# Moving the first attention head's weighted sum from its own period to the period that follows, in a hybrid retention and sparse-attention block

## The chip, the cores and the metric

The kernel runs on one core of one Trainium2 chip. The metric is the time of one execution on the device, in microseconds (us). A profile is one execution recorded by the hardware profiler; its span is the time from its first to its last recorded instruction.

## The reference

One block of a model with 512 tokens, 16 meta tokens ahead of them (528 in all), and 1024 channels, in float32: a gated feed-forward part, a mixer, another gated feed-forward part, and a final norm. The mixer projects its normed input once and feeds two branches, retention with 4 heads and sparse attention with 8 heads of width 128; sigmoid gates merge them. The change lies in the attention branch, which for each head is, cut to what matters:

```python
# per query: the 16 meta tokens, and the 128 keys that an indexer ranks highest
s_meta = einsum('bqhd,bmhd->bhqm', qb, k_meta) * scale
s_sel  = einsum('bqhd,bqkhd->bhqk', qb, k_sel) * scale      # masked where not allowed
p = softmax(concatenate([s_meta, s_sel], axis=-1))
out = einsum('bhqm,bmhd->bqhd', p[..., :16], v_meta) + einsum('bhqk,bqkhd->bqhd', p[..., 16:], v_sel)
```

The queries and keys get a rotary embedding (rope) first. The selection is made once for all heads and stands in the kernel as an additive bias on the scores.

## The kernel before

**Number format and matmuls.** Every float32 operand of a matmul is split into a high part and a low part in a reduced format: ACT (ScalarE) copies the source into the high part, and DVE (VectorE) subtracts it from the source for the low part (`split`, L117 and L118). A product is then three matmuls: high x high, high x low, low x high. Weights go through the same split when they arrive from memory: `raw` is the loaded tile (two buffers), `whi` and `wlo` are its parts (three buffers, used in turn), so a weight split must wait until the matmuls that read the buffer before are done. `mm3` (L157) is the matmul loop of all projections.

**Periods.** The attention branch is one Python loop over eight heads, `for h in range(AH)`. One pass of it is called a period here. In period h TensorE (PE) does, in this order:

1. for h > 0, the scores of head h: 15 matmuls into `psS` (L1970). DVE adds the bias and takes the row maximum (L1973), ACT takes the exponential (L1976), DVE normalises the result in place (`pj`, L1980 and L1981);
2. the query projection (`psaq`) and the key projection (`psak`) of head h + 1. ACT, DVE and POOL (GpSimd) apply rope (L1292 to L1296), and ACT and DVE split the result into `aq` and `ak`, which the scores of the next period read;
3. for h from 2 to 7, the weighted sum of head h - 1 (`weigh_turned`, into `psao`, L2028 and L2029);
4. a projection tile of a gate (`wide_gate`, into `psgate` or `psga`), which has nothing to do with the heads.

**Two ways to turn the probabilities.** The weighted sum needs them with keys on the partitions. For heads 1 to 6, DVE transposes blocks (`turn`), POOL writes them to memory (`pd`), SP (SyncE) reads them back (`land`), and ACT and DVE split them into the parts `pth` and `ptl` (`turned_parts`); this takes so long that the sum comes one period later. Heads 0 and 7 take `transpose_p`: PE transposes into four one-bank PSUM tiles `psPT` (L2037, L2039), and ACT and DVE split those straight into the same buffers `pth` and `ptl`. The 16 rows of the meta tokens go apart into `ptail` (L1367 to L1371). Each of these part buffers exists once.

**Head 0 and head 7.** In period 0 the order on PE is: the two projections of head 1, the transposes of head 0, a gate tile, and then head 0's weighted sum (`weigh_v`: 13 matmuls, L1537 and L1538, and a split into the head's output). Period 7 has the transposes of head 7, a gate tile, and head 7's weighted sum in the same way. `weigh_v` and `weigh_turned` differ in the layout of the parts that they read and write. The output of a head overwrites that head's values in the tile `vo`.

**PSUM.** `sm_tile` has four one-bank tiles, used by `psS` (three of the four score tiles), `psaq`, `psPT` and some gate tiles. `mm_tile` has two two-bank tiles, used by the fourth score tile, `psak`, `psao` and the other gate tiles.

**What sets the order.** PE runs in source order throughout, by `tc.manual_schedule(engines={PE})`. ACT, DVE, POOL and the DMA queues are ordered when the kernel is built, by a planner that fills each engine from the instructions that its own model of the time holds ready, those earlier in the source first. Every engine then works through its queue in that fixed order.

Of the kernel before, what the change touches and what calls it, by code (L numbers as in the profile page):

```python
# [33 lines left out]
AH = 8  # L34
# [47 lines left out]
def kernel(ctx: ExitStack, tc: tile.TileContext, x, meta, g1, wg1, wu1, wd1, gm,  # L82
# [11 lines left out]
    def pool(name, bufs=1, space=None, side=None):  # L94
        kw = {} if space is None else {"space": space}
        if side is not None:
            kw["side"] = side
        return tc.tile_pool(name=name, bufs=bufs, reuse_waits="tile", **kw)
# [17 lines left out]
    def split(src, hi, lo, eng=nc.vector):  # L116
        nc.scalar.activation(hi, src, AF.Copy)  # L117
        eng.tensor_tensor(lo, src, hi.bitcast(F32), ALU.subtract)  # L118
# [459 lines left out]
    def sm_tile(name):  # L578
        return mx["sm"].tile([P, S], F32, tag="sm", name=name)

    def mm_tile(name):
        return mx["mm"].tile([P, 1024], F32, tag="mm", name=name)
# [770 lines left out]
    def split_values(raw, parts):  # L1353

        for c in (0, 2):
            split(raw[:, c : c + 2], *(p[:, c : c + 2, :] for p in parts))
        return [(parts[0][:, c, :], parts[1][:, c, :], tp["v"][:TR, c * P : (c + 1) * P]) for c in range(4)]

    def place_tails(i):

        for r, part in ((0, 0), (32, 0), (64, 1)):
            nc.gpsimd.dma_start(tp["v"][r : r + NM].bitcast(F32).rearrange("q (c d) -> q c d", c=4),
                                vd[i, part].rearrange("(c q) d -> q c d", q=32)[:NM])

    def split_rows(src, t, order):

        nc.scalar.activation(t[:NM], src, AF.Copy)  # L1367
        at = [32 * i for i in range(1, 3) if order[i] == "h"][0]
        nc.scalar.activation(t[at : at + NM], src, AF.Copy)
        at = 32 * order.index("l")  # L1370
        nc.vector.tensor_tensor(t[at : at + NM], src, t[:NM].bitcast(F32), ALU.subtract)  # L1371
# [26 lines left out]
    if True:  # L1398
# [132 lines left out]
        def weighted(ps, vb, prob):  # L1531

            for kb in range(4):
                vh, vl = (part[:, kb * P : (kb + 1) * P] for part in vb[:2])
                ph, pl = prob[kb]
                for i, (a, b) in enumerate(((vh, ph), (vh, pl), (vl, ph))):
                    nc.tensor.matmul(ps[:, KQ[kb] :], a, b, start=kb == 0 and i == 0, stop=False)  # L1537
            nc.tensor.matmul(ps[:, KQ[4] :], vb[2], tp["p"][:TR, :NM], start=False, stop=True)  # L1538
# [371 lines left out]
    with pool("ao") as ao:  # L1910
        vo = [ao.tile([P, AH, S], F32R, tag=f"vo{i}", name="vo") for i in range(2)]
        ao_parts = [(vo[0][:, c, :], vo[1][:, c, :]) for c in range(AH)]
        with pool("at") as at:
# [21 lines left out]
            def proj_q(w=None):  # L1935
                w = w or cq.next()
                ps = sm_tile("psaq")
                mm3([(ps, REAL)], w, xs, KD)
                return rope_q(ps)
# [7 lines left out]
            def proj_k():  # L1947
                w = ck.next()
                parts, ps = halves(mm_tile("psak"))
                mm3(parts, w, xs, KD)  # L1950
                return rope_k(ps)
# [33 lines left out]
            def scores(q, k):  # L1985
                for j in (2, 1, 0, 3):
                    score(j, q, k)()

            def part_tiles(kb, n):
                return [at.tile([P, S - Q0[kb]], F32R, tag=f"pt{c}{kb}", name=f"pt{c}")[:, :n] for c in "hl"]  # L1990

            def turn(h):

                for j in (2, 1, 0, 3):
                    m = min(-(-(NM + P * (j + 1)) // 32), 16)
                    nc.vector.transpose(cross[:, :m, j, :], prob[j][:, : 32 * m].rearrange("p (b k) -> p b k", k=32))
                nc.vector.transpose(crosst, prob[3][:, S : S + 32])
                d = pd[h % 2]
                for a in range(4):
                    nc.gpsimd.dma_start(d.rearrange("(b i) a c -> a i b c", i=32)[a],  # L2000
                                        cross[32 * a : 32 * a + 32].rearrange("p b j c -> p b (j c)"))
                nc.gpsimd.dma_start(land[4], crosst[96 : 96 + NM, NM:])
# [6 lines left out]
            def turned_parts():  # L2009
                parts = []  # L2010
                for kb, q0 in enumerate(Q0):
                    ph, pl = part_tiles(kb, S - q0)
                    split(land[kb], ph, pl)
                    parts.append((ph, pl))
                split_rows(land[4], tp["p"][:, :NM], "hlh")
                return parts

            def weigh_turned(h, parts, v):

                ps = mm_tile("psao")[:, :S]  # L2020
                for kb, q0 in enumerate(Q0):
                    vh, vl = (part[:, kb * P : (kb + 1) * P] for part in v[:2])
                    ph, pl = (part.rearrange("p (a c) -> p a c", a=4) for part in parts[kb])
                    o = ps.rearrange("p (a c) -> p a c", a=4)[:, :, q0 // 4 :]
                    if q0 == 0:
                        (ph, pl), o = parts[kb], ps
                    for i, (a, b) in enumerate(((vh, ph), (vh, pl), (vl, ph))):
                        nc.tensor.matmul(o, a, b, start=kb == 0 and i == 0, stop=False)  # L2028
                nc.tensor.matmul(ps[:, KQ[4] :], v[2], tp["p"][:TR, :NM], start=False, stop=True)  # L2029
                split(*(t.rearrange(f"p ({o}) -> p a j c", a=4, j=4) for o, t in zip(("a j c", "j a c", "j a c"), (ps, *ao_parts[h]))))  # L2030

            def transpose_p():
                parts = []
                for kb in range(4):
                    ps = sm_tile("psPT")
                    for j in range(max(kb - 1, 0), 4):
                        nc.tensor.transpose(ps[:, j * P : (j + 1) * P], prob[j][:, kb * P : (kb + 1) * P], ident)  # L2037
                    if kb == 3:
                        nc.tensor.transpose(ps[:NM, 0:P], prob[3][:, 4 * P : T], ident)  # L2039
                    n = S - KQ[kb]  # L2040
                    ph, pl = part_tiles(kb, n)
                    if kb == 3:
                        split_rows(ps[:NM, P - NM : P], tp["p"][:, :NM], "hlh")
                    split(ps[:, KQ[kb] :], ph, pl)
                    parts.append((ph, pl))
                return parts

            def weigh_v(h, parts, v):
                ps = mm_tile("psao")[:, :S]
                weighted(ps, v, parts)  # L2050
                split(ps, *ao_parts[h])

            def wide_gate(tile=None):
                if gr.at < gr.n:
                    gate_acc(KD - gr.n + gr.at, gate(gr, at, wide=tile is None))
                else:
                    t = gate_a(tile or mm_tile("psga")[:, :S])
                    nc.sync.dma_start(gd[KD + ga.at - 1], t)

            place_tails(4)  # L2060
            with tc.manual_schedule(engines=BUSY):
# [12 lines left out]
                vs = split_values(raw, [v[:, :4, :] for v in vo])  # L2074
                raw = fetch_values(5, vraw())
            pend = None
            for h in range(AH):
                more = h + 1 < AH
                if h:
                    scores(q, k)  # L2080
                if more:
                    q, k = proj_q(w if h == 0 else None), proj_k()
                else:
                    wide_gate(sm_tile("psga"))
                    wide_gate()
                if pend is not None:
                    weigh_turned(h - 1, pend, vs[h - 1])
                    pend = None
                if h == 0:
                    with tc.manual_schedule(engines=BUSY):  # L2090
                        vs += split_values(raw, [v[:, 4:, :] for v in vo])
                    vrs.close()
                    crp = crs.enter_context(pool("cross", 1, side="right"))
                    cross = crp.tile([P, 16, 4, 32], F32, tag="cross", name="cross")
                    for j in range(3):
                        nc.gpsimd.memset(cross[:, 4 * j + 5 :, j, :], 0.0)
                if 0 < h and more:
                    turn(h)
                    wide_gate(sm_tile("psga"))
                    turned(h)  # L2100
                    pend = turned_parts()
                else:
                    pt = transpose_p()
                    wide_gate()
                    weigh_v(h, pt, vs[h])
                if h == 4:
                    place_tails(5)

        crs.close()

# [32 lines left out]
    with pool("om") as ou:  # L2143
# [10 lines left out]
        pend = []  # L2154
        for c in range(KD):
# [5 lines left out]
            if len(pend) == 2:  # L2161
                to_tokens(pend)
                pend = []
            nc.vector.tensor_tensor(hc, ps, hc, ALU.add)
            h, l = new_x(c)
# [248 lines left out]
```

## Time and profile before

| what | value |
|---|---|
| median of 3 runs | 1512.89 us (1512.02 to 1515.25) |
| the profiled execution's own time | 1512.66 us |
| its span | 1510.8 us |
| PE busy | 1498.6 us |
| DVE busy | 1113.5 us |
| ACT busy | 729.9 us |
| POOL busy | 122.2 us |
| mean granted PE clock | 0.997 |
| the loop over the heads, about | 892 to 1068 us of the span |

The rows shown below come from views of this one profiled execution. In the chain of waits a row has a start, a length, and the engine, tile and line that the end of the kernel hung on in that stretch. In the timeline a row has a start, a length, engine, line, operation, output and inputs with their shapes, how many instructions were merged (x), and in brackets the idle time of the engine ahead of it and what ended that. In the windows each stretch has its length and the busy time of each engine, then the granted PE clock, the share of time that the DMA engines were busy, and GB/s. All times are in us from the start of the span.

### The profile page before, as it was taken

The page shows a single profiled execution, that of the slowest core. Times are in us where ns is not written, and L with a number is a line of the kernel's source. Part 1 is how long each engine was busy: PE and PEld are TensorE (multiplying, and loading weights), DVE is VectorE, ACT ScalarE, POOL GpSimd, SP SyncE. Part 2 cuts the span into 40 slices and gives each one's busy share as a digit, 9 for nine tenths or more (in the row PEclk, how much of TensorE's full clock was granted, in tenths as well). Part 3 has the DMA queues.
Part 4 walks back from the last instruction along what each step waited for, and adds up shares of the span by engine and source line. Part 5 has one row for each costly group of instructions (what it writes and reads, how often), then busy time and mean ns, then how long its engine had stood idle before and what let it go on. Part 6 is the DMA issues. An engine that isn't in the chain of part 4 may idle for free.

```text
span 1510.8 us, 23879 instructions
## 1 busy us (share of the span) xinstructions
PE 1498.6 (99%) x9664; PEld 1361.2 (90%) x9664; DVE 1113.5 (74%) x1740; ACT 729.9 (48%) x1134; POOL 122.2 (8%) x169
## 2 busy tenths in 40 slices
PE   9999999999999999999999998999999999999998
PEld 8999999999988888888898887988888899899996
DVE  4988585786786768678978887787455888586675
ACT  5555263454354444443333356677345445254453
POOL 1000000002111120000000132331001000000000
PEclk9999999999999999999999999999999999999999
DMA  5232323226544444232322244566443223233232
GB/s 170 64 121 87 116 92 112 86 96 200 205 149 168 167 146 158 87 122 72 117 93 87 95 130 134 154 189 193 147 135 124 84 84 110 86 112 112 84 117 93
DMA packets 161918, 184.90 MB, mean 122 GB/s; under 512 B 12048, under 2 KB 130344, under 8 KB 161168
## 3 DMA queue, kind: packets, MB, share of 16 engines
q1 hardware_dynamic: 151056, 156.70, 32.3%
q0 software_dynamic: 5920, 17.68, 3.5%
q10 hardware_dynamic: 4832, 9.00, 1.7%
q8 instruction: 76, 1.25, 0.3%
q14 instruction: 34, 0.28, 0.1%
HBM read 161.05 MB, written 22.30 MB: 121 GB/s over the span
## 4 chain that ended last, share of the span: by engine, by line
PE 97%; DVE 1%; ACT 1%; issue 1%; DMA 0%; POOL 0%; POOLq 0%; DVEq 0%; ACTq 0%
PE psqX L157 14%; PE psd L157 8%; PE psd L2249 8%; PE psqY L157 7%; PE psrg L157 6%; PE psro L157 6%; PE psvX L1181 4%; PE psqZ L157 3%; PE psrk L157 3%; PE psu L157 3%; PE psrq L157 3%; PE psga L157 3%; PE psat L157 3%; PE psmo L157 3%; PE psak L157 3%; PE psaq L157 3%
## 5 line engine op out<-in xcount | busy, mean ns | idle before, releaser
L329 ACT ACTIVATE whi<-raw 128x1024 fp32r<-128x1024 f32 (+2 forms) x184 | 169.5, 924 | 129.0 <-PE psd L157 37.5
L330 DVE TENSOR_TENSOR wlo<-raw,whi 128x1024 fp32r<-128x1024 f32 (+2 forms) x184 | 198.6, 1083 | 40.6 <-ACT whi L329 40.5
L157 PE MATMUL psqX<-th,whi 128*128 128x264 f32 (+1 forms) x432 | 122.3, 283 | 0.0
L157 PE MATMUL psqX<-tl,whi 128*128 128x264 f32 (+1 forms) x432 | 122.3, 283 | 0.0
L157 PE MATMUL psqX<-th,wlo 128*128 128x264 f32 (+1 forms) x432 | 122.2, 283 | 0.0
L329 ACT ACTIVATE whi<-wsum 128x1024 fp32r<-128x1024 f32 x72 | 76.3, 1060 | 70.7 <-PE psd L2249 22.0
L117 ACT ACTIVATE whi<-raw 128x1024 fp32r<-128x1024 f32 (+1 forms) x60 | 62.2, 1043 | 86.0 <-PE psat L157 26.6
L330 DVE TENSOR_TENSOR wlo<-wsum,whi 128x1024 fp32r<-128x1024 f32 x72 | 87.8, 1221 | 12.5 <-ACT whi L329 12.5
L118 DVE TENSOR_TENSOR wlo<-raw,whi 128x1024 fp32r<-128x1024 f32 (+1 forms) x60 | 73.6, 1228 | 28.3 <-ACT whi L117 27.4
L157 PEld LDWEIGHTS psqX<-th,whi 128*128 128x128 f32 x432 | 82.1, 190 | 0.1
L157 PEld LDWEIGHTS psqX<-tl,whi 128*128 128x128 f32 x432 | 82.0, 190 | 0.0
L157 PEld LDWEIGHTS psqX<-th,wlo 128*128 128x128 f32 x432 | 82.0, 190 | 0.0
L157 PE MATMUL psro<-vo,whi 128*128 128x512 f32 x256 | 78.7, 389 | 0.0
L157 PE MATMUL psd<-hl,whi 128*128 128x264 f32 x352 | 71.3, 284 | 0.0
L157 PE MATMUL psd<-hh,wlo 128*128 128x264 f32 x352 | 70.8, 283 | 0.0
L157 PE MATMUL psd<-hh,whi 128*128 128x264 f32 x352 | 70.7, 282 | 0.0
L2249 PE MATMUL psd<-wlo,hh 128*128 128x512 f32 (+1 forms) x182 | 69.2, 382 | 0.0
L2249 PE MATMUL psd<-whi,hh 128*128 128x512 f32 (+1 forms) x182 | 69.2, 382 | 0.0
L2249 PE MATMUL psd<-whi,hl 128*128 128x512 f32 (+1 forms) x182 | 69.2, 382 | 0.0
L157 PEld LDWEIGHTS psro<-vo,whi 128*128 128x128 f32 x256 | 48.0, 188 | 10.1 <-DVE vo L330 0.2
L157 PEld LDWEIGHTS psd<-hh,wlo 128*128 128x128 f32 x352 | 54.5, 188 | 0.0
L157 PEld LDWEIGHTS psd<-hh,whi 128*128 128x128 f32 x352 | 54.2, 188 | 0.0
(476 smaller groups left out, 4540.8 us busy)
## 6 DMA issues: line engine op xcount, KB each, us to landing
raw<-in_ffn_w_up_dram SPq DMA_DIRECT2D x22, 1024.0 KB, 5.0
raw<-in_ffn_w_gate_dram SPq DMA_DIRECT2D x21, 1024.0 KB, 5.0
raw<-in_w_in_dram SPq DMA_DIRECT2D x18, 1024.0 KB, 5.0
raw<-in_w_in_dram SPq DMA_DIRECT2D x33, 512.0 KB, 3.8
raw<-in_ffn_w_down_dram SPq DMA_DIRECT2D x24, 512.0 KB, 4.4
w<-in_w_in_dram SPq DMA_DIRECT2D x24, 512.0 KB, 6.1
raw<-in_ffn_w_down_dram SPq DMA_DIRECT2D x12, 768.0 KB, 4.4
raw<-in_w_ret_out_dram SPq DMA_DIRECT2D x8, 1024.0 KB, 4.8
```

Of the source, the lines that this page charges most:

```text
L117: nc.scalar.activation(hi, src, AF.Copy)
L118: eng.tensor_tensor(lo, src, hi.bitcast(F32), ALU.subtract)
L157: nc.tensor.matmul(o, a[:, k, :], b[:, sl], start=first and k == 0 and i == 0, stop=last and k == nk - 1 and i == 2, skip_group_check=onto)
L329: nc.scalar.activation(hi, src, AF.Copy)
L330: return lambda: nc.vector.tensor_tensor(lo, src, hi.bitcast(F32), ALU.subtract)
L1181: nc.tensor.matmul(d[bank_][t], a, b[:, k, :], start=not onto and j + k + m == 0, stop=j + k == 3 and m == 2, skip_group_check=onto)
L2249: nc.tensor.matmul(ps, a[:, bs], m[:, j, cs], start=first and i == 0, stop=last and i == 2)
```

## The change

The parts that `transpose_p` returns in period 0 are no longer used at once; they are kept in `pend`, as the parts of heads 1 to 6 are. In period 1 `weigh_v` for head 0 then stands where `weigh_turned` stands in the later periods: behind the scores of head 1 and the two projections of head 2, ahead of the transposes by DVE and the gate tile. Head 7 keeps its place: its sum is now written behind the loop, and PE reaches it behind the same gate tile as before.

```diff
                 if pend is not None:
-                    weigh_turned(h - 1, pend, vs[h - 1])
-                    pend = None
+                    (weigh_turned, weigh_v)[h == 1](h - 1, pend, vs[h - 1])
...
                     pend = turned_parts()
                 else:
-                    pt = transpose_p()
+                    pend = transpose_p()
                     wide_gate()
-                    weigh_v(h, pt, vs[h])
                 if h == 4:
                     place_tails(5)
+            weigh_v(AH - 1, pend, vs[AH - 1])
```

## The prediction

> **What bounds the kernel now.** I read the page first, for the engine that sets the time.
>
> ```profile
> span 1510.8 us, 23879 instructions
> PE 1498.6 (99%) x9664; PEld 1361.2 (90%) x9664; DVE 1113.5 (74%) x1740; ACT 729.9 (48%) x1134; POOL 122.2 (8%) x169
> PE 97%; DVE 1%; ACT 1%; issue 1%; DMA 0%; POOL 0%; POOLq 0%; DVEq 0%; ACTq 0%
> ```
>
> TensorE carries 97% of the chain that ended last, so an edit that removes no matmul can gain only where PE stands still or runs slowly. The windows show where that is around the moved step.
>
> ```profile
> core 0: us, PE busy (x) PEld busy (x) DVE busy (x) ACT busy (x) POOL busy (x), PEclk, DMA share, GB/s
> 910.00:914.00 4.00, 2.40 (x13) 1.93 (x12) 3.94 (x7) 3.77 (x5) 0.86 (x4) 1.00 0.03 6
> 914.00:920.00 6.00, 5.75 (x26) 5.23 (x27) 4.40 (x20) 4.38 (x10) 1.16 (x1) 0.72 0.61 171
> 935.00:938.00 3.00, 0.65 (x3) 0.22 (x2) 1.84 (x2) 2.97 (x4) 0.00 (x0) 1.00 0.24 54
> 938.00:960.00 22.00, 22.00 (x130) 19.85 (x131) 15.21 (x40) 13.76 (x26) 6.99 (x8) 1.00 0.57 159
> ```
>
> Three losses stand here: PE idle before 914, a granted clock (PEclk) of 0.72 from 914 to 920, and PE idle again between 935 and 938. From 938 on PE is full. The chain of waits names what PE stood for, and also gives an undisturbed period (951 to 980) to compare with.
>
> ```profile
> 911.50 2.36 DVE wlo L118 x2
> ...
> 914.76 2.85 PE psS L1970 x15
> 917.61 6.31 PE psaq L157 x24
> 923.93 5.77 PE psak L157 x48
> 929.70 5.26 PE psgate L157 x23
> ...
> 934.98 1.06 ACT whi L117
> ...
> 937.97 2.10 PE psS L1970 x14
> ...
> 951.29 2.26 PE psao L2028 x12
> 953.56 5.56 PE psga L157 x24
> 959.12 2.02 PE psS L1970 x15
> 961.14 5.47 PE psaq L157 x24
> ...
> 1065.75 1.99 PE psao L1537 x12
> ```
>
> **The change, part by part.** PE runs in source order throughout, so the move happens there for certain. ACT, DVE and POOL are ordered by the planner, and their new order is what I have to guess. In period 0 PE now goes from the gate tile straight to the scores of head 1; in period 1 the weighted sum of head 0 stands between the key projection and the gate tile, which is the shape that periods 2 to 6 have.
>
> *Removed, term 1: the wait inside the sum.*
>
> ```profile
> 910.49 0.40 PE L1537 MATMUL psao<-pth,vo 128*128 128x512 f32 x1
> 914.25 0.39 PE L1537 MATMUL psao<-ptl,vo 128*128 128x256 f32 x1 [1.85 <-DVE ptl L118]
> ```
>
> PE starts the sum at 910.49 and stops for 1.85 us, because the last part of the transposed probabilities lacks its low half. DVE did two weight splits (from 911.50, 2.36 us) ahead of that low half. Moved behind the projections the sum reads parts that are long complete. Gain 1.85.
>
> *Removed, term 2: the slow clock after it.* The scores of head 1 took 2.85 against 2.02 one period later, and the query projection 6.31 against 5.47: 0.83 + 0.84 = 1.67. The window gives the same: 6 x (1 - 0.72) = 1.68. The drop follows the only long wait in its neighbourhood, so I book it to that wait: gain 1.67. A drop does not follow every wait: 2.35 us of idle time between 935 and 938 (3.00 less 0.65 busy), cut in two by one matmul, left the clock at 1.00.
>
> The Trainium skill ("TensorE: Matmul & The Clock Gate", section "HAM oscillation — how this bites in real kernels") states the rule as no idle gap over about 3.4 us. By it a gap of 1.85 us would not slow PE, the 1.67 would have another cause, and the sum would be 1.67 smaller. The trace differs, with a mean of 0.72 granted over the 6 us behind a gap of 1.85.
>
> *Removed, term 3: the wait before the scores of head 2.*
>
> ```profile
> 936.63 0.45 PE L1970 MATMUL psS<-ak,aq 128*128 128x400 f32 x1 [1.45 <-ACT ak L117]
> 935.95 0.63 ACT L117 ACTIVATE ak<-tmp 128x528 fp32r<-128x528 f32 x1
> 956.17 0.64 ACT L117 ACTIVATE ak<-tmp 128x528 fp32r<-128x528 f32 x1 [1.64 <-DVE tmp L1296]
> 956.85 0.71 DVE L118 TENSOR_TENSOR ak<-tmp,ak 128x528 fp32r<-128x528 f32 x1 [0.71 <-ACT ak L117]
> 958.92 1.06 ACT L117 ACTIVATE whi<-raw 128x1024 fp32r<-128x1024 f32 x1 [2.11 <-PE psga L157]
> ```
>
> PE ended the gate tile at 929.70 + 5.26 = 934.96 and got the full keys at 937.97; one of the 15 score matmuls ran in between (2.02 / 15 = 0.13). The loss is 3.01 - 0.13 = 2.88. Its cause is ACT's order: the weight split at 934.98, which waits for the gate tile, stood ahead of the key split (935.95). In the following period, where a weighted sum (2.26) lies between projection and gate tile, ACT does the keys first (956.17), they are complete at 956.85 + 0.71 = 957.56, and the scores start at 959.12 without a wait. There 6.3 us pass from the end of the key projection (951.29) to the complete keys. After the change the cover is 1.99 + 5.56 = 7.55, so 1.3 are left over. Gain 2.88; if that cover failed it would cost up to the same 2.88 again.
>
> The three terms: 1.85 + 1.67 + 2.88 = 6.40. As a check, PE needed 27.48 from 910.49 to 937.97. The same work at undisturbed durations is 1.99 + 2.02 + 5.47 + 5.77 + 5.56 = 20.81, less 6.67, and 0.13 off again for the score matmul already done: 6.54.
>
> *Moved.* The sum issues 13 matmuls with 13 weight loads, one ACT copy and one DVE subtraction, and no DMA; nothing of it is on SP or POOL.
>
> ```profile
> L117 ACT ACTIVATE vo<-psao x8: 597/598/600, 914.8 to 1067.8; 128x512 fp32r<-128x512 f32 x8
> L118 DVE TENSOR_TENSOR vo<-psao,vo x8: 679/690/694, 916.0 to 1068.4; 128x512 fp32r<-128x512 f32 x8
> 940.42 0.20 ACT L1367 ACTIVATE ptail<-land 16x16 fp32r<-16x16 f32 x1
> ```
>
> The matmuls cost the same 1.99 in the new place. The 0.60 on ACT and 0.69 on DVE land between the key rope's steps, where periods 2 to 6 have theirs beside PE work: nothing, by the 1.3 us left over above. The parts of head 0 live longer, and their single buffers are next written by head 1's parts; the first such write stands at 940.42, while the moved sum ends near 910.49 + 2.02 + 5.47 + 5.77 + 1.99 = 925.7. Even 6.4 us earlier that write is over 8 us behind it: no wait.
>
> *Added, term 4: banks for the scores and the query projection.* The four one-bank PSUM tiles are all held by transposed probabilities when the scores of head 1 start at 910.49 instead of 914.76. Its second and third tiles need banks drained by the two low halves at 910.36 to 911.28 (the first row below), about when PE reaches them. The query projection of head 2, due at 910.49 + 2.02 = 912.51, needs the first score tile reduced or the last transposed part drained.
>
> ```profile
> 910.36 0.92 DVE L118 TENSOR_TENSOR ptl<-psPT,pth 128x400 fp32r<-128x400 f32 x2
> 915.45 0.57 DVE L1973 CUSTOM_DVE_ANT_0 tmp<-psS,bias 128x400 f32<-128x400 f32 x1 [1.26 <-PE psS L1970]
> ```
>
> If DVE takes the reduction (0.57) at once at 911.50, the wait is nothing. Behind one weight split (2.36 / 2 = 1.18) it ends at 913.25, a wait of 0.74. Behind both splits and the last low half, which freed PE at 914.25, it is 1.74. A gain is excluded, since no PE work goes away. I take 0.7: the first split is ready before the reduction, and the second is behind it in the source. A gap of 0.7 is nearer to the two short gaps at 936, which left the clock alone, than to 1.85.
>
> Sum against the profiled execution, 1512.66 us (the span of 1510.8 and 1.86 around it, 0.23 under the median of 1512.89): 1512.66 - 6.40 + 0.70 = 1506.96. With 97% of the whole chain on PE, the shift should reach the end whole.
>
> **Rivals.**
>
> 1. *Both splits first.* DVE repeats the order of before and the wait is only exchanged: 1.74 at the query projection, and the slow clock (1.67) comes back with a gap that long. For it: the planner did put both ahead of the low half. Against: the reduction now competes and precedes both in the source. Time: 1512.66 - 6.40 + 3.41 = 1509.7, or 1508.0 where the clock holds.
>
> 2. *The clock drop stays,* because the wait was not its cause: 1506.96 + 1.67 = 1508.6. For it: 2.35 us of idle time at 935 did no harm. Against: the drop sits right behind the longest single gap here. The rule of the Trainium skill named above would make it so.
>
> 3. *Head 1's exchange through memory comes late.* Its parts are now wanted 5.7 us earlier than 951.29, at 945.6.
>
> ```profile
> 927.39 1.31 POOL L2000 DMA_DIRECT2D pd<-cross  x2
> 933.16 0.67 POOL L2000 DMA_DIRECT2D pd<-cross  x1
> 944.64 0.85 DVE L118 TENSOR_TENSOR ptl<-land,pth 128x384 fp32r<-128x384 f32 x2
> ```
>
> They were complete at 944.64 + 0.85 = 945.49. If nothing of the exchange moved, that would just do; it should move with the key rope, behind which its fourth store stands (933.16). If that store slips by one more POOL turn (933.16 - 927.39 = 5.8), PE waits about 5.8 and pays the clock (1.67): 1506.96 + 7.5 = 1514.4.
>
> 4. *The other side: ACT's order tips in every period.* If the planner now puts the weight split that waits for the gate tile ahead of the key split, as it did at 934.98, in periods 1 to 6, term 3 stays and comes five times more: 1512.66 - 1.85 - 1.67 + 0.70 + 5 x 2.88 = 1524.2. It decides from the point where the gate tile ends, in the plan, before the key rope's last DVE step. Against it: in the period shown ACT was idle for 2.11 us between the two, and the shape of those periods does not change.
>
> **How the numbers follow.** Forecast 0.67, rival 1 0.12, rival 2 0.06, rival 3 0.06, rival 4 0.09. The predicted time is the forecast's, 1507.0. About 0.2% (3.0 us) is what a measurement of this kernel can tell from no change. Faster by more than that are the forecast, rival 2 and a third of rival 1: 0.77. Within it lie the rest of rival 1 and rival 3: 0.14. Slower is rival 4: 0.09. The low end is all of 6.40 without term 4, 1506.3, less 0.6 as the fastest run of before lies under the profiled one (1512.02): 1505.7. The high end takes in rival 1 with about 1.3 of spread, 1511.0, and leaves out rivals 3 and 4 (0.15).
>
> **What would show it.** In the new profile: no idle time in front of the moved sum, and its matmuls between the key projection and the gate tile of period 1 (term 1); a granted clock of 1.00 through the scores and query projection that follow the transposes (term 2); the key split ahead of the weight split on ACT, and scores of head 2 that start as the gate tile ends (term 3); before the query projection of head 2 a gap of 0 to 1.74, released by a reduction or a low half on DVE (term 4); and a distance of about 21 us between the scores of heads 1 and 2, where 959.12 - 937.97 = 21.15 is that of the next period. The prediction is wrong if PE shows a new gap over 2 us anywhere from period 1 on, or if the loop's gain does not reach the end.

## The result, and the profile after

| | before | changed |
|---|---|---|
| median of 6 runs, taken together | 1512.55 us (1511.53 to 1515.25) | 1507.55 us (1506.86 to 1510.24) |
| the profiled execution | 1512.66 us, span 1510.8 | 1510.24 us, span 1508.2 |
| PE busy | 1498.6 us | 1498.2 us |

The ratio is 0.9968, with a 95% interval of 0.9955 to 0.9980: 5.0 us faster, where 5.7 was forecast. The profiled execution of the changed kernel is the longest of its six. Most of what made it long is in its chain of waits:

```profile
902.03 7.05 DMA vraw<-vst
...
914.59 1.21 DVE wlo L118
915.80 0.48 DVE tmp L1973
...
916.35 5.74 PE psaq L157 x24
922.09 5.77 PE psak L157 x48
927.86 1.99 PE psao L1537 x12
929.84 0.01 PE psao L1538
929.85 5.58 PE psgate L157 x24
935.43 2.02 PE psS L1970 x15
937.45 5.47 PE psaq L157 x24
```

From 916.35 on every row is PE, end to start. The sum (`psao` at L1537) stands between the key projection and the gate tile, the scores of head 2 start as the gate tile ends (929.85 + 5.58 = 935.43), and scores and query projection take 2.02 and 5.47, the undisturbed durations. Ahead of that stands something new: the second half of the values took 7.05 us to land, and the low halves of head 0's parts wait behind its split. Timeline and windows show what PE lost there, and what the clock did:

```profile
912.44 0.62 PE L1970 MATMUL psS<-ak,aq 128*128 128x400 f32 x2 [0.29 <-DVE ak L118]
914.06 1.72 PE L1970 MATMUL psS<-ak,aq 128*128 128x272 f32 x12 [0.99 <-DVE ptl L118]
916.35 0.50 PE L157 MATMUL psaq<-xh,whi 128*128 128x512 f32 x1 [0.57 <-DVE stat L1973]
914.00:920.00 6.00, 5.37 (x28) 4.55 (x29) 5.90 (x22) 5.94 (x12) 1.66 (x4) 1.00 0.31 87
935.00:938.00 3.00, 3.00 (x21) 2.80 (x20) 1.99 (x9) 2.74 (x3) 0.00 (x0) 1.00 0.38 113
```

PE stops three times around the scores of head 1: for the low half of the keys, for a bank that a late low half (`ptl`) still held, and for the first score tile to be reduced. The granted clock (third number from the right) stays at 1.00, and 935 to 938 is full.

### The profile page after: what moved, and what is told of

It is laid out like the page before. It is cut to its first block, busy times and chain, and to the rows that moved or that the text cites. A ratio compares the mean times of both kernels' runs of the same rounds, so it can differ in the third digit from the quotient of the medians.

```text
span 1508.2 us, 23880 instructions
## 1 busy us (share of the span) xinstructions
PE 1498.2 (99%) x9664; PEld 1359.7 (90%) x9664; DVE 1112.7 (74%) x1740; ACT 729.7 (48%) x1134; POOL 122.2 (8%) x169
## 4 chain that ended last, share of the span: by engine, by line
PE 97%; DVE 1%; DMA 1%; ACT 1%; issue 0%; POOL 0%; POOLq 0%; ACTq 0%; DVEq 0%
PE psqX L157 14%; PE psd L157 8%; PE psd L2248 8%; PE psqY L157 7%; PE psrg L157 6%; PE psro L157 6%; PE psvX L1181 4%; PE psqZ L157 3%; PE psrk L157 3%; PE psu L157 3%; PE psrq L157 3%; PE psga L157 3%; PE psat L157 3%; PE psmo L157 3%; PE psak L157 3%; PE psaq L157 3%
```

## The experiments

The kernel before ran again beside each group: 1513.55 us (median of 19 runs) for the first four, 1513.35 us (of 20) for the rest.

### The changed kernel again

No edit.

> The changed kernel once more, to see an execution that is not the one profiled (1510.24 us, the longest of six, in which the second half of the values landed 7.1 us after its issue, where 5.3 had passed before the change). Theory: the three losses are gone and only the wait for a PSUM bank is left; with values that land in about 5.3 us PE waits about 0.7 us between the gate tile of period 0 and the query projection of head 2, and the time is near 1507.0, 5.7 below the kernel before. Rival: the late values are no accident of that execution but come with the change, because the sum's move shifts the queue of loads; then PE waits about 2.7 us there again and the time is 1509 to 1510.

Measured: 1507.5 us (1507.1 to 1508.04), ratio 0.9962 (0.9949 to 0.9974). The values landed 5.3 us after their issue. PE, DVE and the chain of waits:

```profile
913.70 0.50 PE L157 MATMUL psaq<-xh,whi 128*128 128x512 f32 x1 [0.57 <-DVE stat L1973]
911.92 1.23 DVE L118 TENSOR_TENSOR wlo<-raw,whi 128x1024 fp32r<-128x1024 f32 x1
913.07 0.57 DVE L1973 CUSTOM_DVE_ANT_0 tmp<-psS,bias 128x400 f32<-128x400 f32 x1
929.72 0.65 ACT L117 ACTIVATE ak<-tmp 128x528 fp32r<-128x528 f32 x1 [1.58 <-DVE tmp L1296]
930.39 0.71 DVE L118 TENSOR_TENSOR ak<-tmp,ak 128x528 fp32r<-128x528 f32 x1
932.59 1.06 ACT L117 ACTIVATE whi<-raw 128x1024 fp32r<-128x1024 f32 x1 [2.23 <-PE psgate L157]
927.21 5.58 PE psgate L157 x24
932.79 2.02 PE psS L1970 x15
```

One wait is left, 0.57 us at the query projection: DVE did one weight split (911.92) and then the reduction (913.07), the middle one of the three orders that term 4 weighed. ACT does the key split (929.72) ahead of the weight split (932.59), and the keys are whole at 931.10, 1.7 us before the scores at 932.79. The query projection starts 2.65 us earlier than in the profiled execution (913.70 against 916.35), where the transposes had started only 0.67 earlier. So the longer waits of the profiled execution came with the late values, not with the move.

### The sum behind the scores only

```diff
                 if h:
                     scores(q, k)
+                if h == 1:
+                    weigh_v(0, pend, vs[0])
+                    pend = None
...
-                    (weigh_turned, weigh_v)[h == 1](h - 1, pend, vs[h - 1])
+                    weigh_turned(h - 1, pend, vs[h - 1])
```

> The sum of head 0 goes only behind the scores of head 1, ahead of the projections, so that period 1 has no sum between its key projection and its gate tile. Theory (three separate losses): terms 1 and 2 are gone, about 3.5 us less about 0.7 for the bank; of term 3 the cover is the gate tile alone, 5.56 us, against 6.3 for the key rope, so 0.7 is left if ACT does the key split ahead of the weight split, and all of 2.88 if not: 1508 to 1510 us, slower than the full move by 0.7 to 2.9. Rival (the gain is the head start of the scores alone, and the cover by the sum does nothing): the same time as the full move, 1507.

Measured: 1509.49 us (1508.92 to 1510.08), ratio 0.9975 (0.9965 to 0.9984), 2.0 above the full move. Its waits on PE, and the last matmul of the gate tile ahead of the scores of head 2:

```profile
914.43 0.50 PE L1537 MATMUL psao<-pth,vo 128*128 128x512 f32 x1 [1.14 <-ACT gate L1384]
933.10 0.39 PE L157 MATMUL psgate<-xh,wlo 128*128 128x512 f32 x1
934.26 2.08 PE L1970 MATMUL psS<-ak,aq 128*128 128x400 f32 x14 [0.29 <-DVE ak L118]
```

The wait for the low half is gone. In its place the sum waits 1.14 us for its two-bank PSUM tile, which the sigmoid (L1384) has yet to empty; behind the projections, in the changed kernel, it waits for no tile. ACT did the key split ahead of the weight split that waits for the gate tile here, but the cover of one gate tile was short: the tile ends at 933.10 + 0.39 = 933.49, undisturbed scores (2.02) would end at 935.51, and they end at 934.26 + 2.08 = 936.34, 0.8 us lost. So the cover by the sum does count here, and the place behind the projections is better than the one behind the scores for two reasons, of which the bank had not been foreseen. The profiled execution, the fastest of the nine, is 1.4 us above the profiled one of the changed kernel above, as the two losses less its 0.57 come to; what the others lost beyond that was not seen.

### The key split ahead of the weight split, nothing moved

The kernel before with one edge added; `keys` holds the ACT instruction of each head's key split.

```diff
-                    wide_gate(sm_tile("psga"))
+                    with tc.issue_after(keys[2].ins) if h == 2 else ExitStack():
+                        wide_gate(sm_tile("psga"))
```

> The kernel before, with one edge added: in period 2 the weight split on ACT that waits for the gate tile of period 1 is queued behind the key split of head 2. Nothing moves on PE. Theory (term 3 is ACT's order): terms 1 and 2 stay, the wait before the scores of head 2 falls from 2.9 to about 0.7, the time by about 2.1 us to 1510.5. Rival (term 3 is the missing cover by a sum, and the order on ACT is only what happened to stand there): the wait stays above 2 us and the time stays within 0.7 us of 1512.6.

Measured: 1513.47 us, ratio 0.9999 (0.9990 to 1.0008): no gain. By its time the rival was right; ACT's timeline and the waits of PE tell another story:

```profile
934.11 0.60 ACT L1384 ACTIVATE gate<-psgate 128x512 f32<-128x512 f32 x1 [2.11 <-PE psgate L157]
934.60 0.64 ACT L117 ACTIVATE ak<-tmp 128x528 fp32r<-128x528 f32 x1
914.73 0.39 PE L1537 MATMUL psao<-ptl,vo 128*128 128x256 f32 x1 [1.93 <-DVE ptl L118]
935.29 0.45 PE L1970 MATMUL psS<-ak,aq 128*128 128x400 f32 x1 [1.22 <-ACT ak L117]
936.68 3.42 PE L1970 MATMUL psS<-ak,aq 128*128 128x400 f32 x14 [0.94 <-DVE ak L118]
```

The planner put another instruction that waits for the gate tile, its sigmoid, in the place of the weight split. The keys still came late, so this run did not test the order; the next but one does.

### The kernel before again, for the clock

No edit, one execution.

> The kernel before once more, for its profile. Question: where does the slow clock fall? Theory of the prediction (the drop belongs to the wait of 1.85 us inside the sum): the granted clock falls below 1.00 right behind that wait again and nowhere else in the loop. Rival (the drop comes when a stretch of about 3.4 us on a clock of its own is about half idle, so that either of the two waits can bring it, or neither, from one execution to the next): the drop may stand behind the wait before the scores of head 2 instead, or be absent, with 1.6 us for each drop.

Measured: 1513.56 us. Its two waits (the second is in two pieces, 1.45 and 0.89), and two windows:

```profile
914.53 0.39 PE L1537 MATMUL psao<-ptl,vo 128*128 128x256 f32 x1 [1.92 <-DVE ptl L118]
936.67 3.42 PE L1970 MATMUL psS<-ak,aq 128*128 128x400 f32 x14 [0.89 <-DVE ak L118]
934.00:938.00 4.00, 1.78 (x7) 1.52 (x8) 2.36 (x4) 3.95 (x5) 0.73 (x1) 0.87 0.28 66
938.00:942.00 4.00, 4.00 (x19) 3.59 (x19) 2.83 (x16) 3.71 (x12) 0.54 (x1) 0.70 0.99 306
```

The same program, the same two waits, and the slow stretch is behind the other one: the 14 score matmuls at 936.67 take 3.42, where the first profile has 2.10, and the lost clock is 4 x 0.13 + 4 x 0.30 = 1.72 us. Behind the wait of 1.92 there is none. What the rival foresaw came: either wait can bring the drop. Its mechanism is not shown by that.

### Both gate-tile instructions behind the key split, nothing moved

The edge from above, and a second one for the sigmoid of period 1.

```diff
+        with tc.issue_after(keys[2].ins) if len(keys) == 3 else ExitStack():
             nc.scalar.activation(t, ps, AF.Sigmoid)
```

> The kernel before, with both instructions on ACT that wait for the gate tile of period 1 (its own sigmoid, and the weight split of period 2) queued behind the key split of head 2. Nothing moves on PE. Theory (term 3 is ACT's order; with one of the two queued behind, the other had taken its place): the wait before the scores of head 2 falls to what the cover of 5.56 us lacks of the rope's 6.3, about 0.7, from 2.9; the time falls by 2.1 us, and by up to 1.6 more where the slow clock had stood behind that wait: 1509.9 to 1511.4 against 1513.5. Rival (the cover by a sum is what counts): the wait stays above 2 us and the time is 1512.8 to 1513.6.

Measured: 1510.65 us (1508.87 to 1513.96), ratio 0.9980 (0.9971 to 0.9989): 2.7 us less. From the chain of its profile, whose values landed after 7.5 us, and from the timelines of ACT and PE:

```profile
902.09 7.47 DMA vraw<-vst
...
938.58 0.72 DVE ak L118
...
939.34 2.08 PE psS L1970 x14
```

```profile
932.12 0.64 ACT L117 ACTIVATE aq<-tmp 128x512 fp32r<-128x512 f32 x1 [2.13 <-DVE tmp L1296]
938.70 0.40 PE L157 MATMUL psgate<-xh,wlo 128*128 128x512 f32 x1
```

The gate tile ends at 938.70 + 0.40 = 939.10, undisturbed scores would end at 941.12, and they end at 939.34 + 2.08 = 941.42: 0.3 us are lost instead of 2.88. Term 3 was the order of ACT's queue.

### The values last, nothing moved

The kernel before, with the block that splits the second half of the values, and makes the `cross` tile in their memory, written behind the transposes and the gate tile.

```diff
-                if h == 0:
-                    with tc.manual_schedule(engines=BUSY):
-                        vs += split_values(raw, [v[:, 4:, :] for v in vo])
...
                     pt = transpose_p()
                     wide_gate()
+                    if h == 0:
+                        with tc.manual_schedule(engines=BUSY):
+                            vs += split_values(raw, [v[:, 4:, :] for v in vo])
...
                     weigh_v(h, pt, vs[h])
```

> The kernel before, with the split of the second half of the values written behind the transposes and the gate tile of period 0. DVE then drains the last part ahead of the two weight splits. Nothing moves on PE. Theory (term 1 is DVE's order): the wait of 1.85 us inside the sum falls below 0.5, no slow clock behind it, term 3 stays: 1.4 to 3.1 us less, 1510.4 to 1512.1 against 1513.5. Rival (the last part is late by its own chain over ACT and DVE, whatever stands beside it): the wait stays above 1.3 us and the time within 0.6 us.

Measured: 1511.29 us (1509.19 to 1512.21), ratio 0.9985 (0.9976 to 0.9994): 2.1 us less. In the chain, on DVE, and on PE:

```profile
905.93 5.49 PE psgate L157 x24
911.43 2.21 PE psao L1537 x12
912.66 0.42 DVE L118 TENSOR_TENSOR ptl<-psPT,pth 128x256 fp32r<-128x256 f32 x1
912.99 2.35 DVE L118 TENSOR_TENSOR wlo<-raw,whi 128x1024 fp32r<-128x1024 f32 x2
933.93 0.45 PE L1970 MATMUL psS<-ak,aq 128*128 128x400 f32 x1 [1.45 <-ACT ak L117]
935.28 3.56 PE L1970 MATMUL psS<-ak,aq 128*128 128x400 f32 x14 [0.90 <-DVE ak L118]
```

DVE does the last low half ahead of both weight splits, and the sum follows the gate tile without a stop (2.21 against 1.99 undisturbed): term 1 was the order of DVE's queue. Term 3 is untouched, and the slow stretch stands behind it (3.56).

### Both queue orders mended, nothing moved

The edits of the last two together.

> The kernel before with both edits: the values last, and the key split of head 2 ahead of the sigmoid and the weight split. The sum of head 0 stays in its own period. Theory (the whole gain of the move is two bad queue orders and the slow clock that their waits bring): both waits are nearly gone, no slow clock is left, and the time is within 1 us of the changed kernel: 1507.5 to 1508.5. Rival (the place of the sum on PE counts for itself): a gain of at most half of the move's, 1510.5 or more.

Measured: 1507.52 us (1507.04 to 1508.03), ratio 0.9961 (0.9948 to 0.9974), the time of the move itself. What is left of the two waits, with the last matmul of the gate tile:

```profile
913.24 0.39 PE L1537 MATMUL psao<-ptl,vo 128*128 128x256 f32 x1 [0.19 <-DVE ptl L118]
932.20 0.40 PE L157 MATMUL psgate<-xh,wlo 128*128 128x512 f32 x1
...
932.85 2.10 PE psS L1970 x14
```

There are 0.19 us left ahead of the sum's last part and 0.3 at the scores (932.60 + 2.02 = 934.62, against 934.95), where the changed kernel has its 0.57 at the query projection. So once both orders are mended, the place of the sum on PE makes no difference that these runs show. The gain is the two waits and the clock. Mended alone they give 2.1 and 2.7, 4.8 in sum; together 5.8. The 1.0 us more (4.8 against 5.8) fits a drop that goes only when no wait of that size is left.

### The changed kernel with the values last

The block moved in the same way in the changed kernel.

> The changed kernel, with the split of the second half of the values (and the cross tile that takes the memory of the loaded values) written behind the transposes and the gate tile of period 0 instead of ahead of them; the parts of head 0 no longer queue behind it on ACT and DVE. Theory (what is left between the gate tile and the query projection is banks whose draining waits behind the value split): all parts but the last drain earlier, the wait there falls to between 0 and 0.6 us, also where the values land late, and the time is 0 to 0.7 us below the changed kernel in its usual executions. Rival (the key split of head 1, which now queues behind a value split too, or the shifted order later in the loop, costs more than the banks gave): the scores of head 1 start later and the time is 0.5 to 2 us above the changed kernel.

Measured: 1507.33 us (1506.82 to 1507.51), ratio 0.9961 (0.9947 to 0.9974). The chain has PE alone through period 0:

```profile
905.64 5.50 PE psgate L157 x24
911.14 2.02 PE psS L1970 x15
913.15 5.50 PE psaq L157 x24
```

The last wait is gone from the trace, 0.57 us. Against 1507.5 on the same chip the 0.17 of the medians is inside both spreads, so it is not shown to be faster than the changed kernel. That it would also stay clear of late values is likely from its order, and was not seen, since here they landed after 5.3 us.

## Why the prediction was right

- **Term 1 (1.85).** Right, in size and cause. The sum waits for nothing in its new place, and the wait was DVE's order, as the values-last kernel shows without moving anything.
- **Term 2 (1.67).** The size was right, the reason only in part. A drop costs 1.68 to 1.72 in the profiles of the kernel before, but it does not belong to the wait inside the sum; in the second profile it stood behind the other. The sum came out since the move takes both waits away, which is luck as far as this term goes. Had it removed the first alone, as the values-last kernel does, this term would have been counted too surely. Rival 2, where the drop stays because no wait causes it, is ruled out by the profiles of the changed kernel, with 1.00 throughout. The rule of the Trainium skill weighed there ("TensorE: Matmul & The Clock Gate", section "HAM oscillation — how this bites in real kernels"), a gap of about 3.4 us, is again not borne out: no gap of PE in the loop is that long in these profiles, and the drops are there.
- **Term 3 (2.88).** Right. ACT's order tipped, as in the periods that served as the pattern, and 1.7 us of the cover were left over where 1.3 were forecast. The 934.96 in its working is the end of the 23rd of the gate tile's 24 matmuls; the last ends at 934.78 + 0.39 = 935.17, and measured by the end of the scores (937.97 + 2.10 = 940.07, against 935.17 + 2.02 = 937.19) the loss is 2.88 all the same. Without the sum as cover a lack of 0.7 was expected; it was 0.8 with the sum behind the scores and 0.3 with the orders mended. From the end of the key projection to the whole keys 6.3 us pass in the pattern (951.29 to 957.56), 6.2 in the first of these (928.01 to 934.22) and 5.7 in the second (933.61 to 939.30, its last matmuls running from 933.21 for 0.40). The difference of 0.6 is as long as the query split on ACT (0.62), which stands behind the end of the key projection in the first two (at 952.05 and 928.78) and ahead of it in the third (at 932.12).
- **Term 4 (0.7).** Right in the usual execution: 0.57, by the order that was held for likeliest. What it lacked is that the same bank waits grow when the values land late. That made 0.29 + 0.99 + 0.57 = 1.85 in the profiled execution, none of it followed by a drop.
- **The moved instructions** cost nothing, as forecast. Rivals 3 and 4 did not come: ACT kept its order in period 1, and from 916 us on the chain is PE alone through the sum of head 1. Behind the query projection of head 2 neither profile of the changed kernel has any idle time of PE in the loop.
- **The sum.** From the first transposes to the key projection of head 3 PE needed 36.30 us in the second profile of the changed kernel (903.97 to 940.27), and 42.24 in the second one of the kernel before:

```profile
903.97 1.42 PE psPT L2037 x13
940.27 5.77 PE psak L157 x48
```

```profile
903.55 1.42 PE psPT L2037 x13
945.79 5.77 PE psak L157 x48
```

That is 5.94 against 5.70 forecast. The medians differ by 5.0 in the first set of runs and by 6.05 in the second: the kernel before moved by 1.0 from one set to the next, the changed one by 0.05.

## What to carry to other kernels

Where an engine runs in a fixed queue, look for the instruction that stands ahead of the late one, and not only for the late one itself: here weight splits that PE needed only 10 to 19 us later (923.93 and 929.70 after 914.25, 953.56 after 934.98) held up what it needed next. A step of PE work can be placed so that it covers another engine's chain, but mending the two queue orders gave the same time, so price both before moving work. When one such instruction is pushed back, check that the planner doesn't put another with the same wait in its place.

## What the runs showed of the hardware

A wait of PE has a second price that is paid only sometimes. The kernel with both gate-tile instructions behind the key split shows it at its deepest, a granted clock of 0.50. Because its values landed late, PE stopped twice inside the sum there:

```profile
914.55 0.45 PE L1537 MATMUL psao<-ptl,vo 128*128 128x400 f32 x1 [1.53 <-DVE ptl L118]
917.82 0.58 PE L1537 MATMUL psao<-ptl,vo 128*128 128x256 f32 x1 [1.73 <-DVE ptl L118]
914.00:918.00 4.00, 1.72 (x7) 1.26 (x8) 3.70 (x7) 3.33 (x5) 1.30 (x4) 0.66 0.11 19
918.00:922.00 4.00, 4.00 (x17) 3.99 (x18) 1.90 (x9) 2.73 (x5) 0.71 (x1) 0.50 0.85 243
```

At a clock of 0.50 the 1.72 us lost in the second profile of the kernel before are a stretch of about 3.4 us. Here 4 x 0.34 + 4 x 0.50 = 3.4 us of clock are missing, a stretch about twice as long, and the second wait lies inside it. A drop stood behind a wait of 1.85 once, behind 1.45 + 0.89, 1.22 + 0.94 and 1.45 + 0.90 in three other profiles, behind the 1.53 above, and not behind 1.92, 1.93 or the first profile's 1.45 + 0.89. The length of the wait alone does not decide, then. A clock of its own that judges every 3.4 us by whether PE was about half idle would roughly fit these cases; this was argued from them and not tried by itself, and the share at which it would tip isn't known. The Trainium skill ("TensorE: Matmul & The Clock Gate", section "Part 1: The HAM clock gate (the "warmup" mystery)") states a free-running window of 3413 ns; the length of the slow stretch agrees with it. The spread of the times is in line with a drop that comes only sometimes: 1512.0 to 1515.5 and 1509.2 to 1512.2 for the kernel before and the one with the values last, 1.0 us or less for the changed kernel in its second set and for the one with both orders mended, though these two have only five runs each.

The load of the values, 1 MB with the same queue order, landed after 5.2 to 5.5 us in most profiles and after 7.1 and 7.5 in two, and both of those executions were the longest of their kernel's runs.
